# Where the modulation vectors are multiplied: from filler products of the tensor engine to VectorE accumulations

## Chip, core and metric

The kernel runs on one core of a Trainium2 chip. The metric is the device time of one execution in microseconds (us). The core has engines that run side by side and wait for one another by semaphores: TensorE (PE: products; PEld: its weight loads), VectorE (DVE), ScalarE (ACT), GpSimd (POOL), and SyncE (SP), which here issues all DMAs, in order.

## The reference

Two blocks of two layers each run over 256 tokens of 1024 channels, in float32. The first block has a pooling mixer, stick-breaking attention and two squared-relu MLPs. The second has windowed attention and differential attention, two more MLPs, and a context of 256 tokens. Every layer of the second block is modulated by vectors made from `c` and `c_ctx`:

```
for i in range(DEPTH):
    need_ctx = i < DEPTH - 1
    mod_x = jax.nn.silu(c) @ w_ada[i] + b_ada[i]
    mod_c = jax.nn.silu(c_ctx) @ w_ada[i] + b_ada[i]
    sh1, sc1, g1, sh2, sc2, g2 = jnp.split(mod_x[:, None, :], N_MOD, axis=-1)
    csh1, csc1, cg1, csh2, csc2, cg2 = jnp.split(mod_c, N_MOD, axis=-1)
    hx = x * (1.0 + sc1) + sh1
    hc = ctx * (1.0 + csc1) + csh1
...
```

`w_ada[i]` is 1024 x 6144, 25 MB for each of the two layers: two vectors times a large matrix. The change is in this product alone.

## The kernel before

Weights come from DRAM in blocks of 1 MB as two `raw` tiles (three buffers). ACT rounds a block to `whi`, DVE subtracts to make `wlo` (three buffers each), and PE multiplies activations, split in the same way, by three products for each pair (`mm`, L607). `mmf` (L613) is a product in full float32, `tr` (L637) a transpose by `ident`. An MLP has 16 blocks of hidden columns; for each, PE runs 48 products of 256 columns (up) and 24 of 512 columns (down), and ACT and DVE make the squared relu in `c` tiles between them.

The order of instructions on PE, DVE, ACT and POOL is decided when the program is built. Everything that PE does is written as *lanes*, generators that yield until an event, an instruction or a PSUM bank is there. `weave` runs the lanes, the first ready one first, with a table of costs for every engine; the other engines' instructions wait in lists and are laid down by the time at which they could start, less urgent ones (`urgent`) only if they are ready enough earlier. On the chip, each engine then runs its list strictly in order. All instructions of DVE, ACT, POOL and SP pass through one helper, so the profile shows them all at L109. Where PE would have nothing to do for more than 1 us, `keep_warm` lays down a product of `ident` with itself that nobody uses.

The product silu(c) @ w_ada was not a lane. `setup_rest` puts silu(c) and silu(c_ctx) into two of 32 columns of `cT` and queues two generators `ada(0)` and `ada(1)` as *fillers*. A filler step takes two `adaw` tiles (128 rows x 1024 columns of w_ada, 512 KB each, four buffers) and runs four products of 32 x 512 with `cT` as weights, each into its own quarter of one PSUM bank, summed over eight row blocks. `weave` takes a filler step where PE has a gap of over 300 ns, or where a step is due: `mlp` raises `due` after certain blocks (`F0`, `F1`, `F2`). There are 2 layers x 3 banks x 8 row blocks = 48 steps. After each bank, `ada_end` adds the bias, writes the gates to DRAM, transposes and fills `modT`, and marks the events `mod0.0` to `mod1.5`.

Of the kernel before, what the change touches and what calls it, by code (L numbers as in the profile page):

```python
# [11 lines left out]
F32 = mybir.dt.float32  # L12
# [8 lines left out]
P = 128  # L21
D = 1024
T = 256
# [10 lines left out]
# rows of the table of vectors that are laid along the partitions  # L34
# [21 lines left out]
FILL = 1000  # L56
# [4 lines left out]
# the gap of the tensor engine that is filled to keep its clock up; when it starts, and until when its clock is low  # L61
WARM = 1000
START, COLD = 1100, 6000
# how many fillers ahead of their time, and in which gaps
SPARE, GAP = -99, 300
# [4 lines left out]
F0, F1 = range(3, 15), range(2, 14)  # L70
F2 = {c: 2 for c in range(2, 14)}


class Unit:
    """to yield: a filler's next unit of work, once ops are through"""

    def __init__(self, ops):
        self.ops = ops


class Banks:
    """to yield: n PSUM banks are free, of the most that may be taken"""
# [5 lines left out]
class Op:  # L88
    """an instruction of an engine: what it waits for, what it takes, and when it ends (None: not laid down yet)"""
# [5 lines left out]
class Engine:  # L95
    """Stands for an engine: its calls are kept until the order of the engine's instructions is decided."""
# [58 lines left out]
class Net:  # L155
    """Everything that the tensor engine does is written as lanes: generators that yield after a few products, with the
    time until the lane's next products can start, the name of an event that it waits for, or the number of PSUM banks that
    it keeps between its steps. weave() runs the lanes, the
    first ready one first, and so lays down the tensor engine's order."""

    def __init__(self, ctx, tc, a, out):
# [19 lines left out]
        self.fill = deque()  # L181
        self.fill_at, self.fill_last, self.fill_wait, self.due = 0.0, 0.0, 0.0, 0
# [4 lines left out]
    def region(self, ap):  # L187
        """the name of what ap lies in, and its columns there as bits"""
# [53 lines left out]
    def ready(self, op):  # L242
        """when op can start for what it waits for; None: not known yet"""
# [14 lines left out]
    def first_op(self):  # L258
        """the instruction that starts next, (start, engine, op), of all engines"""
# [16 lines left out]
    def start(self, op, t, e):  # L276
        """when e can start op, which is ready at t; two engines don't go to a PSUM bank at once"""
# [28 lines left out]
    def settle(self, op):  # L306
        """lays down instructions until op is"""
# [30 lines left out]
    def done(self, *aps):  # L338
        """to yield: what lays aps down"""
# [18 lines left out]
    def fill_step(self):  # L358
        self.due -= isinstance(self.fill_wait, Unit)
        r = self.step(self.fill[0], 1)  # L360
        if r is None:
            self.fill.popleft()
        self.fill_last, self.fill_at, self.fill_wait = self.now, self.now + FILL, 0.0 if r is None else r

    def can_fill(self):
        t = self.when(self.fill_wait) if self.fill and self.now >= self.fill_at else None
        return t is not None and t <= self.now

    def when(self, r):
        """when a lane that yielded r goes on; None: not known yet"""  # L370
# [4 lines left out]
        if isinstance(r, Unit):  # L375
            r = r.ops
# [18 lines left out]
    def weave(self, lanes):  # L395
        lanes = [[g, 0.0] for g in lanes]
        while lanes:
            self.catch_up()
            self.sweep()
            if self.can_fill() and (self.due > 0 or not isinstance(self.fill_wait, Unit)):  # L400
                self.fill_step()
                continue
# [8 lines left out]
            else:  # L411
                if self.can_fill() and self.due > SPARE and (nxt is None or nxt - self.now > GAP):
                    self.fill_step()
                    continue
                n = self.first_op()
                ts = [t for t in (nxt, n and n[0], self.fill_at if self.fill and self.fill_at > self.now else None,
                                  self.when(self.fill_wait) if self.fill else None) if t is not None and t > self.now]
# [6 lines left out]
            r = self.step(e[0], 1 if e[0].__name__ in ("gemms", "setup_rest") else 0)  # L424
# [7 lines left out]
    def keep_warm(self):  # L432
        """a product that nobody asks for: the tensor engine's clock halves when it has been idle for some microseconds"""
# [11 lines left out]
    def need(self, name):  # L445
        while name not in self.ev:
            self.due = max(self.due, 1)
            yield 500

# [5 lines left out]
    def t(self, tag, cols, bufs, dt=F32):  # L455
        t = self.base.tile([P, cols], dt, name=self.uid(tag), tag=tag, bufs=bufs)
        if tag in ("raw", "adaw", "whi", "wlo"):
# [25 lines left out]
    def free(self, *banks):  # L483
        """nothing more will be asked of them"""
# [25 lines left out]
    def wide(self, src):  # L510
        """a vector in DRAM on every partition"""
# [42 lines left out]
    def block(self, key, w, c0, uses=1):  # L554
        """columns c0.. of w [1024, n] -> [128, 8, 256]"""
# [7 lines left out]
    def rows(self, key, w, c, uses=1):  # L563
        """rows 256 c.. of w [n, 1024] -> [128, 2, 1024]"""
# [50 lines left out]
    def sum3(self, out, l, r, n, last="l"):  # L615
        """out = the sum over k < n of l(k) @ r(k); the low parts of one side are used last"""
# [13 lines left out]
    def pairs(self, parts):  # L630
        """parts: (out, l's two parts, r's) on different rows of the array, in turns"""
# [18 lines left out]
    def meansq2(self, x):  # L650
        """the same of x [128, 1024], on two engines"""
# [5 lines left out]
    def meansq(self, src):  # L657
        """mean of the squares of each row of the two halves of 512 columns, as two parts of a sum"""
# [1365 lines left out]
```

## Time and profile before

| what | before |
|---|---|
| three runs | 1520.4, 1521.74, 1524.77 us |
| median | 1521.74 us |
| span of the profiled execution | 1520.4 us |
| HBM read in it | 257.18 MB |
| w_ada of it: 96 loads of 512 KB | 50.3 MB |

One execution is profiled. "Busy" is the time in which an engine had an instruction running; PE's ends are modelled. A chain of waits follows the work that ended last back to the start. A stretch A:B is a part of the span in us. In a group, "x384" is the number of instructions; a float32 product shows as two records on PE (a product of 32 x 512 likewise), so a filler step of four products shows as eight.

### The profile page before, as it was taken

The page shows a single profiled execution, that of the slowest core. Times are in us where ns is not written, and L with a number is a line of the kernel's source. Part 1 is how long each engine was busy: PE and PEld are TensorE (multiplying, and loading weights), DVE is VectorE, ACT ScalarE, POOL GpSimd, SP SyncE. Part 2 cuts the span into 40 slices and gives each one's busy share as a digit, 9 for nine tenths or more (in the row PEclk, how much of TensorE's full clock was granted, in tenths as well). Part 3 has the DMA queues.
Part 4 walks back from the last instruction along what each step waited for, and adds up shares of the span by engine and source line. Part 5 has one row for each costly group of instructions (what it writes and reads, how often), then busy time and mean ns, then how long its engine had stood idle before and what let it go on. Part 6 is the DMA issues. An engine that isn't in the chain of part 4 may idle for free.

```text
span 1520.4 us, 26084 instructions
## 1 busy us (share of the span) xinstructions
PE 1496.9 (98%) x10346; PEld 1316.7 (87%) x10346; DVE 980.2 (64%) x1939; ACT 744.5 (49%) x1565; POOL 37.8 (2%) x57
## 2 busy tenths in 40 slices
PE   8999999999999999999999999999999999999997
PEld 8878888988988888888799997878889999899996
DVE  7645558667766555888684443435479877885556
ACT  6544446565765554577542322222245544655442
POOL 2000000001000000000000000000000000100001
PEclk9999999999999999999999999999999999999999
DMA  8687778434656767644653234554224322366652
GB/s 291 221 273 275 241 250 277 144 120 149 199 148 217 230 216 235 213 164 137 209 183 98 84 111 162 172 168 165 84 85 138 97 71 84 98 208 193 187 182 90
DMA packets 152109, 261.02 MB, mean 172 GB/s; under 512 B 8985, under 2 KB 113906, under 8 KB 151986
## 3 DMA queue, kind: packets, MB, share of 16 engines
q1 hardware_dynamic: 151986, 259.35, 52.8%
q8 instruction: 81, 1.33, 0.4%
q14 instruction: 42, 0.34, 0.1%
HBM read 257.18 MB, written 2.13 MB: 171 GB/s over the span
## 4 chain that ended last, share of the span: by engine, by line
PE 87%; DVE 5%; DMA 5%; ACT 1%; issue 1%; SPq 0%; POOL 0%; ACTq 0%; DVEq 0%; POOLq 0%
PE b L607 77%; PE b L613 6%; PE b L637 4%; DVE wlo L109 2%; DMA adaw<-in_w_ada_dram 1%; DVE nat L109 1%; DVE c L109 1%; DMA raw<-in_w_up_dram 1%; DVE h L109 1%; DMA c<-in_b_lk_dram 1%; ACT whi L109 1%; DMA raw<-in_a_wq_dram 0%; ACT c L109 0%; DMA raw<-in_pool_w_dram 0%; DMA raw<-in_w_kv_dram 0%
## 5 line engine op out<-in xcount | busy, mean ns | idle before, releaser
L607 PE MATMUL b<-h,whi 128*128 128x256 f32 x3072 | 568.7, 284 | 0.0
L109 ACT CAST whi<-raw 128x512 fp32r<-128x512 f32 x716 | 400.8, 617 | 340.5 <-PE b L607 228.4
L109 DVE TENSOR_TENSOR wlo<-raw,whi 128x512 fp32r<-128x512 f32 x716 | 458.5, 687 | 159.3 <-ACT whi L109 157.7
L607 PE MATMUL b<-whi,c 128*128 128x512 f32 x1536 | 506.5, 396 | 0.0
L607 PEld LDWEIGHTS b<-h,whi 128*128 128x128 f32 x3072 | 483.8, 192 | 6.7 <-ACT c L109 2.5
L607 PE MATMUL b<-h,wlo 128*128 128x256 f32 x1536 | 378.6, 284 | 0.0
L607 PEld LDWEIGHTS b<-whi,c 128*128 128x128 f32 x1536 | 288.6, 188 | 88.2 <-ACT c L109 14.3
L607 PE MATMUL b<-wlo,c 128*128 128x512 f32 x768 | 300.3, 391 | 0.0
L607 PEld LDWEIGHTS b<-h,wlo 128*128 128x128 f32 x1536 | 294.2, 192 | 2.8 <-issue 0.3
L109 ACT ACTIVATE c<-b 128x512 f32<-128x512 f32 (+1 forms) x116 | 64.7, 568 | 226.3 <-PE b L607 224.5
L109 DVE TENSOR_TENSOR c<-c 128x512 f32<-128x512 f32 x80 | 55.2, 691 | 185.5 <-ACT c L109 185.2
L607 PE MATMUL b<-whi,h 128*128 128x256 f32 x896 | 170.6, 287 | 3.1 <-DVE c L109 2.7
L607 PEld LDWEIGHTS b<-wlo,c 128*128 128x128 f32 x768 | 144.6, 188 | 25.1
L607 PEld LDWEIGHTS b<-whi,h 128*128 128x128 f32 x896 | 141.8, 192 | 5.7 <-ACT c L109 3.7
L109 DVE TENSOR_TENSOR c<-b,c 128x512 f32<-128x512 f32 (+3 forms) x121 | 71.5, 597 | 99.4 <-PE b L607 69.6
L607 PE MATMUL b<-wlo,h 128*128 128x256 f32 x432 | 110.3, 288 | 0.0
L607 PEld LDWEIGHTS b<-wlo,h 128*128 128x128 f32 x432 | 83.6, 193 | 2.4 <-issue 1.5
L109 DVE TENSOR_TENSOR c<-c,c 128x512 fp32r<-128x512 f32 (+3 forms) x122 | 75.6, 633 | 8.2 <-ACT c L109 0.6
L109 ACT COPY c<-b 128x512 f32<-128x512 f32 (+1 forms) x78 | 44.9, 582 | 52.7 <-PE b L637 33.7
L637 PE MATMUL b<-ident,c 128*128 128x128 f32 x434 | 64.2, 275 | 3.4 <-DVE c L109 2.2
L109 ACT ACTIVATE c<-c 128x512 fp32r<-128x512 f32 (+1 forms) x112 | 64.7, 603 | 2.2
L637 PEld LDWEIGHTS b<-ident,c 128*128 128x128 f32 x434 | 49.3, 140 | 15.8 <-issue 5.5
(130 smaller groups left out, 982.0 us busy)
## 6 DMA issues: line engine op xcount, KB each, us to landing
raw<-in_mlp_w_dram SPq DMA_DIRECT2D x128, 512.0 KB
adaw<-in_w_ada_dram SPq DMA_DIRECT2D x96, 512.0 KB
raw<-in_w_up_dram SPq DMA_DIRECT2D x64, 512.0 KB
raw<-in_w_down_dram SPq DMA_DIRECT2D x64, 512.0 KB
raw<-in_w_kv_dram SPq DMA_DIRECT2D x16, 512.0 KB
raw<-in_a_wq_dram SPq DMA_DIRECT2D x16, 512.0 KB
raw<-in_a_wo_dram SPq DMA_DIRECT2D x16, 512.0 KB
raw<-in_w_q_dram SPq DMA_DIRECT2D x8, 512.0 KB
```

The source lines that it names most:

```text
L109: op, way = Op(), (self.cost(f, out, reads, kw), lambda: getattr(self.real, f)(out, *args, **kw))
L607: self.product(30 if free else max(n, 256) / 2.4 + 3, out, (l, r), lambda: self.pe.matmul(out, l, r, start=start, stop=stop, **k))
L613: self.product(30 if free else max(n, 128) / 0.6 + 4, out, (l, r), lambda: self.pe.matmul(out, l, r, start=start, stop=stop, **k))
L637: self.product(109, out, (src, self.ident), lambda: self.pe.transpose(out, src, self.ident))
```

## The change

The filler steps go, with `due`, `Unit`, `fills` and all that belongs to them. `ada` becomes a lane, which starts when `setup_rest` is through. For every 128 x 1024 tile of w_ada, DVE multiplies the tile by silu(c) of its row (one value for each partition) and adds it to an accumulator `acc`, and again for silu(c_ctx): at layer 1 only the first two of the six vectors are made for the context as well. After eight tiles an accumulator holds, on each partition, the sum over the row blocks. For each pair of vectors PE then sums over the partitions, by products with `rowsel`, whose column r is all ones. The `adaw` tiles have three buffers instead of four, `acc` has four, and a scratch area that is reserved for DMAs is made smaller to make room. DVE's instructions for it have urgency 3 (a smaller number goes first; the weights' roundings have 2, and less when their block is next).

```diff
         self.set_lam()
-        self.fill.extend(self.ada(i) for i in range(2))
-        self.fill_at = self.now + 8000
+        self.rowsel = c.tile([P, 2, 32], F32, name="rowsel")
+        nc.vector.memset(self.rowsel, 0.0)
+        for r in range(2):
+            nc.vector.memset(self.rowsel[:, r, r:r + 1], 1.0)
+        self.mark("ada")
...
-            raw = raws.popleft()
-            for jj in range(2):
-                j = 2 * i + jj
-                self.mmf(bank[32 * j:32 * j + 32, :], self.cT[:, k, :], raw[:, jj * 512:jj * 512 + 512], k == 0, k == 7, free=j > 0)
...
+                if k == 0:
+                    acc = [self.t("acc", 1024, 4) for _ in range(2 if layer == 0 or m < 2 else 1)]
+                    accs.append(acc)
...
+                raw = raws.popleft()
+                with self.urgent(ADAP):
+                    for r, t in enumerate(acc):
+                        g = self.cT[:, k, r:r + 1]
+                        if k == 0:
+                            nc.vector.tensor_scalar(t, raw, g, None, ALU.mult)
+                        else:
+                            nc.vector.scalar_tensor_tensor(t, raw, g, t, ALU.mult, ALU.add)
+                if n + ADAW < len(steps):
+                    raws.append(load(*steps[n + ADAW]))
+                if m % 2 == 0 or k < 7:
+                    yield self.done(*acc)
+                    continue
+                yield self.done(*acc), Banks(1)
                 bank = self.bank()
...
+                for r in range(len(acc)):
+                    for j in range(4):
+                        self.mmf(bank[32 * j:32 * j + 32, :], self.rowsel[:, r, :], accs[j // 2][r][:, j % 2 * 512:j % 2 * 512 + 512],
+                                 r == 0, r == len(acc) - 1, free=j > 0)
+                yield from self.ada_end(layer, m // 2, bank, bias)
...
-            self.due += fills.get(c, 0)
...
-            if self.can_fill() and (self.due > 0 or not isinstance(self.fill_wait, Unit)):
-                self.fill_step()
-                continue
...
-    nc = bacc.Bacc("TRN2", target_bir_lowering=False, num_devices=1)
+    nc = bacc.Bacc("TRN2", target_bir_lowering=False, num_devices=1, dynamic_dma_scratch_size=1024)
```

Since the costs in `weave` decide the order, it moves everywhere. Three places show it.

PE in the first MLP, at the down products of one block, before (`b_658` and `b_659` are accumulators, `b_962` the fillers' bank; "x2" are equal rows):

```order
L607 MATMUL b_658<-whi_1406,c_1404 128x512
L607 MATMUL b_658<-wlo_1407,c_1404 128x512
L607 MATMUL b_658<-whi_1406,c_1405 128x512
L613 MATMUL b_962<-adaw_1297,cT 32x512 x2
L613 MATMUL b_962<-adaw_1300,cT 32x512 x2
L607 MATMUL b_659<-whi_1406,c_1404 128x512
L607 MATMUL b_659<-wlo_1407,c_1404 128x512
```

And now (`mm` is at L573 of the changed kernel):

```order
L573 MATMUL b_658<-whi_1401,c_1399 128x512
L573 MATMUL b_658<-wlo_1402,c_1399 128x512
L573 MATMUL b_658<-whi_1401,c_1400 128x512
L573 MATMUL b_659<-whi_1401,c_1399 128x512
L573 MATMUL b_659<-wlo_1402,c_1399 128x512
```

The filler step is gone from between the products. In its stead there are, at one place of this MLP, two rows for each of `acc_843`, `acc_1384`, `acc_844` and `acc_1385` with `rowsel`.

DVE in the first MLP before, two blocks (`wlo` of the weights, then the two `c` rows of the squared relu):

```order
L109 TENSOR_TENSOR wlo_1823<-raw_1824,whi_1822 128x512 x2
L109 TENSOR_TENSOR wlo_1823<-raw_1825,whi_1822 128x512 x2
L109 TENSOR_TENSOR c_1883<-c_1882 128x512
L109 TENSOR_TENSOR c_1885<-c_1883,c_1884 128x512
L109 TENSOR_TENSOR wlo_1887<-raw_1888,whi_1886 128x512 x2
L109 TENSOR_TENSOR wlo_1887<-raw_1889,whi_1886 128x512 x2
```

And now (all of DVE's instructions are at L98 of the changed kernel):

```order
L98 TENSOR_TENSOR c_1752<-c_1750,c_1751 128x512
L98 SCALAR_TENSOR_TENSOR acc_1385<-adaw_1484,cT,acc_1385 128x1024
L98 TENSOR_TENSOR wlo_1754<-raw_1755,whi_1753 128x512 x2
L98 TENSOR_TENSOR wlo_1754<-raw_1756,whi_1753 128x512 x2
L98 SCALAR_TENSOR_TENSOR acc_1384<-adaw_1582,cT,acc_1384 128x1024
L98 SCALAR_TENSOR_TENSOR acc_1385<-adaw_1582,cT,acc_1385 128x1024
L98 SCALAR_TENSOR_TENSOR acc_1384<-adaw_1657,cT,acc_1384 128x1024
L98 TENSOR_TENSOR wlo_1798<-raw_1799,whi_1797 128x512 x2
L98 TENSOR_TENSOR wlo_1798<-raw_1800,whi_1797 128x512 x2
L98 TENSOR_TENSOR c_1864<-c_1863 128x512
```

Four accumulations stand among the ten instructions of a block. Of the 160 in all, 49 are laid down among the `wlo` that belong to 60 to 240 us of the profile before, 33 among those of 240 to 390, 53 of 390 to 600, 9 of 600 to 770 and 16 at the start of the third MLP. Layer 1's begin beside the second MLP and end early in the third; the last filler step before starts at 1067 us, near the third MLP's end.

PE at the end of the first MLP before (the last down product, then the transposes of the normalised activations for keys, values and queries):

```order
L607 MATMUL b_661<-whi_2292,c_2358 128x512
L613 MATMUL b_1787<-adaw_2137,cT 32x512 x2
L613 MATMUL b_1787<-adaw_2140,cT 32x512 x2
L637 MATMUL b_2496<-ident,c_2424 128x128 x4
L637 MATMUL b_2506<-ident,c_2425 128x128 x4
L613 MATMUL b_1787<-adaw_2254,cT 32x512 x2
L613 MATMUL b_1787<-adaw_2257,cT 32x512 x2
L637 MATMUL b_2527<-ident,c_2515 128x128 x4
```

And now (L579 with `ident` alone is a keep-warm product, L603 a transpose):

```order
L573 MATMUL b_661<-whi_2290,c_2358 128x512
L579 MATMUL b_2494<-ident 128x128
L579 MATMUL b_2496<-ident 128x128
L579 MATMUL b_2500<-ident 128x128
L579 MATMUL b_2502<-ident 128x128
L579 MATMUL b_2504<-ident 128x128
L579 MATMUL b_2507<-ident 128x128
L579 MATMUL b_2512<-ident 128x128
L579 MATMUL b_2514<-ident 128x128
L579 MATMUL b_2517<-ident 128x128
L603 MATMUL b_2522<-ident,c_2429 128x128 x4
L603 MATMUL b_2529<-ident,c_2430 128x128 x4
```

Where filler steps stood, nine keep-warm products stand before the transposes, and four more follow until the stage is under way: 13, against one before. In the whole program they are 69 against 58.

More of the change, by code (lines that the diff above doesn't have):

```diff
@@ L62 @@
 WARM = 1000
+ADAW, ADAP = 3, 3
 START, COLD = 1100, 6000
-SPARE, GAP = -99, 300
 LATE = {"so": 2, "co": 2, "xo": 2, "do": 2}
 FIN = lambda tok, ks: [(h, k) for h in range(2) for k in ks] if tok else [(h, k) for k in ks for h in range(2)]
[L70 to L78, printed above, removed]
 class Banks:
@@ L356, in urgent @@
         self.prio = old
[L358 to L367, printed above, removed]
     def when(self, r):
@@ L411, in weave @@
             else:
-                if self.can_fill() and self.due > SPARE and (nxt is None or nxt - self.now > GAP):
-                    self.fill_step()
-                    continue
                 n = self.first_op()
-                ts = [t for t in (nxt, n and n[0], self.fill_at if self.fill and self.fill_at > self.now else None,
-                                  self.when(self.fill_wait) if self.fill else None) if t is not None and t > self.now]
+                ts = [t for t in (nxt, n and n[0]) if t is not None and t > self.now]
                 assert ts, [e[1] for e in lanes]
@@ L423, in weave @@
                 continue
-            r = self.step(e[0], 1 if e[0].__name__ in ("gemms", "setup_rest") else 0)
+            r = self.step(e[0], 1 if e[0].__name__ in ("gemms", "setup_rest", "adas") else 0)
             if r is None:
@@ L456, in t @@
         t = self.base.tile([P, cols], dt, name=self.uid(tag), tag=tag, bufs=bufs)
-        if tag in ("raw", "adaw", "whi", "wlo"):
+        if tag in ("raw", "adaw", "acc", "whi", "wlo"):
             old = self.tags.setdefault(tag, [])
@@ L735, in mask, with ada @@
         return mk
[L738 removed]
+    def ada(self):
         nc = self.nc
[L740 to L770 removed]
@@ new lines, in ada, with load @@
+        for layer in range(2):
+            w = self.a["w_ada_2"][layer].rearrange("(k p) f -> p k f", p=P)
+            b = self.a["b_ada_2"][layer]
+            steps = [(m, k) for m in range(6) for k in range(8)]
+            def load(m, k):
+                raw = self.t("adaw", 1024, ADAW)
+                nc.sync.dma_start(raw, w[:, k, m * 1024:m * 1024 + 1024])
+                return raw
+            raws = deque(load(*s) for s in steps[:ADAW])
+            for n, (m, k) in enumerate(steps):
+                if m % 2 == 0 and k == 0:
+                    accs = []
+                    bias = self.c()
+                    nc.vector.memset(bias, 0.0)
+                    bv = b[m * 1024:m * 1024 + 2048].rearrange("(j f) -> j f", f=512)
+                    for j in range(4):
+                        nc.sync.dma_start(bias[32 * j:32 * j + 2, :], bv[j:j + 1, :].broadcast_to((2, 512)))
+                if k == 0:
+                    acc = [self.t("acc", 1024, 4) for _ in range(2 if layer == 0 or m < 2 else 1)]
+                    accs.append(acc)
+                    for t in acc:
+                        self.uses[t.name] = 2
+                raw = raws.popleft()
[12 more added lines that the diff above has]
+                yield self.done(*acc), Banks(1)
+                bank = self.bank()
+                for r in range(len(acc)):
+                    for j in range(4):
+                        self.mmf(bank[32 * j:32 * j + 32, :], self.rowsel[:, r, :], accs[j // 2][r][:, j % 2 * 512:j % 2 * 512 + 512],
+                                 r == 0, r == len(acc) - 1, free=j > 0)
+                yield from self.ada_end(layer, m // 2, bank, bias)
@@ L919, in fold, with mlp @@
         return G, B
-    def mlp(self, name, h, waits, done, fills={}, hc=None, hc_waits=(), cacc=None, extra={}):
+    def mlp(self, name, h, waits, done, hc=None, hc_waits=(), cacc=None, extra={}):
         nc = self.nc
@@ L1839, in gemms @@
             G[1](), G[2]()
-            yield from self.mlp("m0", H["m0"], ("m00", "m01"), done, fills={c: 1 for c in F0})
+            yield from self.mlp("m0", H["m0"], ("m00", "m01"), done)
             self.stickmask = self.mask("stick", 640)
@@ L1848, in gemms @@
             done = residual("m1", a["mlp_post_g"][1])
-            yield from self.mlp("m1", H["m1"], ("m10", "m11"), done, fills={c: 1 for c in F1},
+            yield from self.mlp("m1", H["m1"], ("m10", "m11"), done,
                                 extra={3 * b: [lambda b=b: self.ctx_q(H["hc"], b, st)] for b in (1, 2, 3)})
```

38 lines of the change are left out of this document (5 added, 33 removed).

## The prediction, made before the changed kernel ran

> **What bounds the kernel now.** I read the page first: the shares of the engines and the chain that ended last.
>
> ```profile
> span 1520.4 us, 26084 instructions
> ...
> PE 1496.9 (98%) x10346; PEld 1316.7 (87%) x10346; DVE 980.2 (64%) x1939; ACT 744.5 (49%) x1565; POOL 37.8 (2%) x57
> ...
> PE 87%; DVE 5%; DMA 5%; ACT 1%; issue 1%; SPq 0%; POOL 0%; ACTq 0%; DVEq 0%; POOLq 0%
> ```
>
> The tensor engine (PE) carries 87% of the chain, VectorE (DVE) and the DMAs 5% each. A mean says little about a stage, so next come the chain in order of time (start, length, what) and the engines' busy time in seven stretches, cut at the changes of stage.
>
> ```profile
> 122.13 11.44 PE b L607 x72
> 134.56 11.44 PE b L607 x72
> ...
> 770.52 146.92 PE b L607 x963
> ...
> 1330.47 179.54 PE b L607 x1152
> ```
>
> ```profile
> core 0: us, PE busy (x) PEld busy (x) DVE busy (x) ACT busy (x) POOL busy (x), PEclk, DMA share, GB/s
> 60.00:240.00 180.00, 179.56 (x1151) 146.93 (x1150) 99.14 (x170) 83.02 (x160) 2.19 (x4) 1.00 0.77 255
> 240.00:390.00 150.00, 148.61 (x1136) 135.97 (x1134) 105.37 (x207) 94.93 (x210) 4.02 (x4) 1.00 0.52 164
> 390.00:600.00 210.00, 210.00 (x1492) 180.92 (x1491) 128.71 (x263) 116.38 (x260) 0.00 (x0) 1.00 0.65 205
> 600.00:770.00 170.00, 166.21 (x1221) 139.78 (x1219) 137.43 (x315) 113.74 (x261) 4.96 (x10) 0.99 0.54 181
> 770.00:1120.00 350.00, 350.00 (x2264) 306.79 (x2257) 172.72 (x274) 101.57 (x182) 0.00 (x0) 1.00 0.41 135
> ```
>
> The four MLPs are pure PE time: the last one's 1152 products run in one piece of 179.54 us, 11.22 us for each of 16 blocks of 72. In the first MLP, blocks start 134.56 - 122.13 = 12.43 us apart. The 1.21 us between them are a filler step. DVE stands idle there for 180 - 99.1 = 80.9 us, but only for 44.6 us in the key/value and stick-breaking stretch and 32.6 us in the windowed attention (600 to 770).
>
> **What goes: 48 filler steps of PE.** The group of the steps' products, one step in the first MLP, and the steps in the stretches:
>
> ```profile
> L613 PE MATMUL b<-adaw,cT x384: 592/605/617, 72.7 to 1067.6; 128*32 128x512 f32 x192
> ```
>
> ```profile
> 133.18 0.39 PE L607 MATMUL b<-whi,c 128*128 128x512 f32 x1
> 133.50 1.07 PE L613 MATMUL b<-adaw,cT 128*32 128x512 f32 x8
> 134.49 0.50 PE L607 MATMUL b<-whi,c 128*128 128x512 f32 x1
> ```
>
> ```profile
> 60.00:240.00 180.00, 18.09 (x128) 2.65 (x128) 1.00 0.77 255
> ...
> 390.00:600.00 210.00, 9.59 (x72) 1.41 (x72) 1.00 0.65 205
> 600.00:770.00 170.00, 11.18 (x80) 1.70 (x80) 0.99 0.54 181
> 770.00:1120.00 350.00, 14.37 (x112) 2.04 (x104) 1.00 0.41 135
> ```
>
> The three views are the step's group over the whole run, the timeline round one step, and the steps' share of each stretch. Eight records make a step: 48 in all. From start to start the step holds PE for 134.49 - 133.50 = 0.99 us, and the products on either side are spread by another 0.2 us; the two block pitches give the same sum, 1.21. So 16 steps lie in 60 to 240, 9 in 390 to 600, 9 before 770, and 14 in the third MLP (one of them across the cut at 770). The third MLP runs without a break where it has no steps (146.92 us), so nothing but PE sets its time.
>
> Not all 16 steps of the first stretch are on the path. The last three stand at the MLP's end:
>
> ```profile
> 231.25 1.06 PE L613 MATMUL b<-adaw,cT 128*32 128x512 f32 x8
> 232.25 1.09 PE L637 MATMUL b<-ident,c 128*128 128x128 f32 x8
> 233.27 1.07 PE L613 MATMUL b<-adaw,cT 128*32 128x512 f32 x8
> ...
> 238.17 1.06 PE L613 MATMUL b<-adaw,cT 128*32 128x512 f32 x8
> ```
>
> Transposes of normalised activations stand between them, and the order of the changed kernel has 13 keep-warm products here, where the one before has 1. I take it that these three filled time in which PE had nothing else. So 13 + 9 + 14 = 36 steps count in full: 36 x 1.21 = **43.6 us**. Of the other 12 (at most 14.5 us, at least nothing), the nine in windowed attention stand where DVE is busy 137.4 of 170 us and several engines wait on each other; I count a third of the nine, **3.6 us**, and none of the three.
>
> **What comes to PE.** 40 products of the same shape with `rowsel` as weights, in six groups: 16 records each for layer 0's three groups and layer 1's first, 8 for the other two. That is ten step lengths of 1.00 and six times 0.21 for the edges: **11.3 us**, of which 2.2 us fall to each of the first four groups (one in the first MLP, one in stick-breaking, two in the second MLP). PE's net is 43.6 + 3.6 - 11.3 = 35.9 us.
>
> **What comes to DVE.** 160 instructions on 128x1024: 140 SCALAR_TENSOR_TENSOR and 20 TENSOR_SCALAR. No row of before has that width. The nearest have half and a quarter of it (groups with their mean in ns, and two in a row in the timeline):
>
> ```profile
> L109 DVE SCALAR_TENSOR_TENSOR c<-x,s_rs,wide 128x512 f32<-128x512 f32 x16 | 11.4, 746 | 2.1 <-POOL s_rs L109 2.0
> ...
> L109 DVE SCALAR_TENSOR_TENSOR h<-b,poolg,h 128x256 fp32r<-128x256 f32 x8 | 3.6, 473 | 0.8 <-ACT h L109 0.8
> ```
>
> ```profile
> L109 DVE TENSOR_SCALAR c<-c,s_rz 128x512 f32<-128x512 f32 x20 | 9.3, 482 | 0.3
> ...
> L109 DVE TENSOR_SCALAR c<-c,s_rz 128x256 f32<-128x256 f32 x23 | 7.5, 352 | 0.6
> ```
>
> ```profile
> 26.06 1.41 DVE L109 SCALAR_TENSOR_TENSOR x<-nat,s_rs,x 128x512 f32<-128x512 f32 x2
> ```
>
> Doubling the width again: 746 + 2 x 273 = 1292 ns and 482 + 2 x 130 = 742 ns. Two in a row take 1.41 us, so a neighbour starts after 1.41 - 0.75 = 0.66 us, 0.09 before the end that the record shows. I use 1.20 us (at least twice 0.66 less a start, at most 1.29) and 0.66 us: 140 x 1.20 + 20 x 0.66 = 181 us, DVE's share rising to about 77%.
>
> The order puts them early: 49 beside the first MLP (42 + 7), 33 in 240 to 390 (28 + 5), 53 in 390 to 600 (48 + 5), 9 to 770, 16 at the start of the third MLP. In time 55.0, 36.9 and 60.9 us in the first three. DVE's idle there, with PE's net change taken off, is 80.9 - 13.5 = 67.4, 44.6 + 2.2 = 46.8 and 81.3 - 6.5 = 74.8 us. So 82, 79 and 81% of all idle time has to serve. What the idle consists of (who waited for what: total, times, longest):
>
> ```profile
> DVE c L109 <- ACT c L109: 224.0, 102, 7.1
> ...
> DVE wlo L109 <- ACT whi L109: 157.7, 107, 6.3
> ```
>
> ```profile
> SPq L109 <- DVE wlo L109: 927.9, 317, 22.8
> SPq L109 <- PE b L613: 163.9, 43, 12.5
> ```
>
> Its pieces have means of 2.2 and 1.5 us: one new instruction fits a mean piece, with a rest. That makes three quarters usable, with half and all as ends. A late `wlo` hurts only once PE has used up the weight blocks made ahead (three buffers, 5.6 us of PE each), while in attention PE waits for the `c` behind it. With three quarters, 4.4 + 1.8 + 4.8 = **11.0 us** do not fit; with all nothing; with half 21.3 + 13.5 + 23.5 = 58.3 us. A new wait comes with it: each new instruction waits for its `adaw` load, and behind it in DVE's fixed order stand `wlo` and, in attention, the `c` of the next step, for which PE waits. The sums' own wait, PE for the last accumulation, sits at six places alone; if DVE is late there, that is part of the same sum.
>
> **Queues.** Behind an `adaw` load in SP's queue stand weight loads. Its wait for a buffer was for PE's steps (163.9 us) and is now for two DVE instructions; the queue waits 927.9 us for `wlo` anyway, so I cost it at nothing while DVE keeps up, and it is part of the same 58 us if not. Traffic: 24.5 loads instead of 32 beside the first MLP leave 45.9 - 3.9 = 42.0 MB in 166.5 us, 252 GB/s against 255. The other two stretches rise to some 220 and 235, below what the first sustains. `rowsel`, the bias and the smaller scratch cost nothing here: one-time, or beside idle time of 80.9 us.
>
> **Sum.** 1520.4 - 35.9 + 11.0 = **1495 us**. The span is 1520.4, as is the fastest of the three runs; the median 1521.74 is 0.1% above.
>
> **Rivals.**
> (1) *DVE takes PE's place* (slower). From 60 to 600 us DVE's stream has no room; `wlo` and the attention's `c` come late and PE waits. It decides below a usable share of (152.8 - 35.9) / 189.0 = 62%. At half: 1520.4 - 35.9 + 58.3 = 1543 us; at 55%, 1533. For it: 82% must serve, in a fixed order in which DVE also waits for ACT and for loads. Against: pieces longer than one instruction.
> (2) *Everything hides*, and the steps in attention pay too: 1520.4 - (43.6 + 14.5 - 11.3) = 1474 us.
> (3) *The steps lay in slack* and removing them brings nothing: 1520 us. Against it stand 12.43 and 11.22 us. [...]
> (4) *The clock drops* where no step fills a pause. One drop is in the trace:
>
> ```profile
> 648.00:652.00 4.00, 1.33 (x12) 0.79 (x5) 2.04 (x4) 3.09 (x9) 0.00 (x0) 0.89 0.87 279
> 652.00:656.00 4.00, 4.00 (x26) 4.00 (x26) 3.94 (x9) 3.82 (x10) 0.00 (x0) 0.68 0.83 305
> ```
>
> PE was busy 1.33 of 4 us, then the granted clock read 0.89 and 0.68: 4 x (0.11 + 0.32) = 1.7 us lost. At all 12 places, 20 us: 1515 us. The keep-warm products speak against it. [...]
>
> **Chances.** Forecast (65 to 90% usable, 1480 to 1515): 0.50. Rival 1: 0.24, of which 0.03 lies near the turning point. Rival 2: 0.14. Rival 3: 0.07. Rival 4: 0.05, split over both sides of the bound. About 0.3% (4.6 us) can be told from no change, so faster means below 1517. Faster 0.50 + 0.14 + 0.02 = 0.66; within 0.07 + 0.03 + 0.03 = 0.13; slower 0.21. The range goes from rival 2 to rival 1 at 55%, 1473 to 1533, and leaves out the worse half of rival 1.
>
> **What would show it.** Right: blocks of the first and third MLP 11.2 to 11.6 us apart; DVE near 1.2 us an instruction and over 90% busy from 60 to 600; the third MLP shorter by 16 us. Wrong: PE idle before products with `wlo` or `c`, ended by DVE, adding up to more than 36 us before 640 us (rival 1); blocks still 12.4 us apart (rival 3); more stretches with a clock under 0.9 (rival 4). The forecast also fails if the wide instruction takes much over 1.3 us.

## The result, and the profile after

| kernel | median of its runs | range | ratio to before, 95% interval |
|---|---|---|---|
| before, same chip | 1521.13 us (4 runs) | 1520.4 to 1524.77 | 1 |
| changed | 1480.9 us (4 runs) | 1479.58 to 1481.3 | 0.9727 [0.9713, 0.9741] |

The changed kernel is faster by 40 us, more than the 26 us forecast, and inside the range. One of the seven runs of the kernel before that stood beside e1 to e4 took 1618.24 us at a mean granted clock of 0.85; medians and ratios leave it out. The page of its profiled execution (span, busy time of each engine, shares of the chain that ended last):

```profile
span 1479.5 us, 25724 instructions
...
PE 1452.4 (98%) x10064; PEld 1313.7 (89%) x10064; DVE 1154.4 (78%) x2100; ACT 745.7 (50%) x1567; POOL 38.7 (3%) x57
...
PE 89%; DVE 5%; DMA 3%; ACT 2%; issue 1%; POOL 0%; SPq 0%; ACTq 0%; DVEq 0%; POOLq 0%
```

PE is busy 44.5 us less than the 1496.9 us before, DVE 174.2 us more, and DVE's share of the chain is still 5%: nearly all of the new work lies beside PE's. The same stretches as before:

```profile
core 0: us, PE busy (x) PEld busy (x) DVE busy (x) ACT busy (x) POOL busy (x), PEclk, DMA share, GB/s
60.00:240.00 180.00, 177.19 (x1163) 160.56 (x1162) 166.36 (x243) 91.21 (x171) 3.34 (x4) 1.00 0.79 254
240.00:390.00 150.00, 148.76 (x1119) 132.70 (x1119) 136.85 (x243) 97.66 (x222) 2.49 (x4) 1.00 0.63 204
390.00:600.00 210.00, 208.98 (x1456) 185.62 (x1455) 190.26 (x318) 115.14 (x256) 1.41 (x2) 1.00 0.74 239
600.00:770.00 170.00, 166.17 (x1241) 146.85 (x1241) 157.09 (x334) 115.33 (x261) 4.34 (x8) 1.00 0.51 166
770.00:1120.00 350.00, 349.96 (x2272) 319.74 (x2272) 204.67 (x333) 114.08 (x211) 3.79 (x8) 1.00 0.37 119
```

DVE now runs 91 to 92% of the time from 60 to 600 us, and PE 98% and more beside it. The chain in order of time (start, length, what) has the first and third MLP in whole pieces, where blocks and filler steps took turns before:

```profile
62.53 100.30 PE b L573 x645
...
810.95 274.53 PE b L573 x1752
```

The new instructions by form (least, median and greatest ns; first and last start), and all that PE waited for between 60 and 640 us (total, times, longest):

```profile
L98 DVE SCALAR_TENSOR_TENSOR acc<-adaw,cT,acc x140: 1274/1278/1289, 66.2 to 805.8; 128x1024 f32<-128x1024 f32 x140
...
L579 PE MATMUL b<-acc,rowsel x80: 592/592/617, 162.8 to 807.6; 128*32 128x512 f32 x80
L98 DVE TENSOR_SCALAR acc<-adaw,cT x20: 629/747/754, 64.9 to 789.5; 128x1024 f32<-128x1024 f32 x20
```

```profile
PE b L603 <- DVE c L98: 3.2, 5, 1.0
PE b L573 <- DVE wlo L98: 1.7, 3, 1.2
PE b L573 <- DVE c L98: 1.7, 3, 0.9
```

The durations were sized well (1278 and 747 ns against 1292 and 742; neighbours start 1.20 us apart, as assumed). PE's waits for DVE come to 6.6 us, where 36 would have meant that DVE had become the bound. The keep-warm products, which stand where PE would wait, add little to that: they take 3.6 us from 60 to 700 us, against 0.9 before. PE's 80 records of sums stand in six groups, at 162.8, 286.4, 447.8 and 567.7 us (1.92 us each from first start to last end) and at 727.7 and 807.2 us (1.07 us): 9.8 us in all.

To see where the 41 us of the trace came from, I number the 4608 products of `h` with `whi` or `wlo` that each trace has in the order of their starts, and compare the start of the same product in both. The differences are cumulative; the points are named by the time before.

| point before, us | stage there | changed kernel ahead by | gained since the last point | forecast for it |
|---|---|---|---|---|
| 202 | late in the first MLP | 13.8 | 13.8 | |
| 244 | its end, on to keys and values | 12.1 | -1.7 | 9.1 for both |
| 382 | stick-breaking done | 10.5 | -1.6 | -4.0 |
| 582 | second MLP done | 19.0 | 8.5 | 3.9 |
| 770 | windowed attention done | 25.2 | 6.2 | 1.4 |
| 1101 | third MLP done | 40.6 | 15.4 | 14.5 |

The forecasts are the prediction's terms, each put where its step or sum stands (up to 582: 9 x 1.21 - 2.2 - 4.8 = 3.9). The prediction counted the fourth sum to the second MLP, but it comes after that MLP's last product, so it stands in the row of 770, and so does the step at 769.5 us, the first of the third MLP's 14. One entry is good to about 1.6 us: a second profile of the changed kernel (e11) is ahead by 13.6, 12.2, 10.5, 18.2, 26.0 and 41.2 us at the same points, and one of the kernel before (e10, with the same instructions in the same order) is 1.2 us ahead of the first at 202 us and stays so, since the filler step at 83 us does not wait 1.2 us for its w_ada load there. The third MLP came out nearly as forecast. In the first two MLPs and windowed attention the kernel gained more than forecast, in stick-breaking it lost less. Two suspects: the loss to DVE's late results was set too high, or more of the 48 steps paid than 36.

### The profile page after: what moved, and what is told of

It reads as the page before. It is cut to its first block, busy times and chain, and to the rows that moved or that the text cites. A ratio compares the mean times of both kernels' runs of the same rounds, so it can differ in the third digit from the quotient of the medians.

```text
span 1479.5 us, 25724 instructions
## 1 busy us (share of the span) xinstructions
PE 1452.4 (98%) x10064; PEld 1313.7 (89%) x10064; DVE 1154.4 (78%) x2100; ACT 745.7 (50%) x1567; POOL 38.7 (3%) x57
## 3 DMA queue, kind: packets, MB, share of 16 engines
q1 hardware_dynamic: 151986, 259.35, 54.5%
## 4 chain that ended last, share of the span: by engine, by line
PE 89%; DVE 5%; DMA 3%; ACT 2%; issue 1%; POOL 0%; SPq 0%; ACTq 0%; DVEq 0%; POOLq 0%
PE b L573 81%; PE b L579 4%; PE b L603 3%; DVE c L98 1%; DVE wlo L98 1%; DVE nat L98 1%; ACT c L98 1%; ACT whi L98 1%; DVE h L98 1%; DMA raw<-in_a_wq_dram 1%; DMA raw<-in_pool_w_dram 0%; DMA raw<-in_w_down_dram 0%; DVE s_mx L98 0%; POOL s_rs L98 0%; DMA adaw<-in_w_ada_dram 0%
## 5 line engine op out<-in xcount | busy, mean ns | idle before, releaser
L573 PE MATMUL b<-h,whi 128*128 128x256 f32 x3072 | 568.3, 284 | 0.0
L98 ACT CAST whi<-raw 128x512 fp32r<-128x512 f32 x716 | 403.2, 618 | 313.1 <-PE b L573 177.8
L98 DVE TENSOR_TENSOR wlo<-raw,whi 128x512 fp32r<-128x512 f32 x716 | 458.3, 687 | 53.8 <-ACT whi L98 52.4
L573 PE MATMUL b<-whi,c 128*128 128x512 f32 x1536 | 497.1, 393 | 0.9 <-DVE c L98 0.9
L573 PEld LDWEIGHTS b<-h,whi 128*128 128x128 f32 x3072 | 483.7, 192 | 5.3 <-issue 1.8
L573 PE MATMUL b<-h,wlo 128*128 128x256 f32 x1536 | 379.4, 284 | 0.0
L573 PEld LDWEIGHTS b<-whi,c 128*128 128x128 f32 x1536 | 288.6, 188 | 63.7 <-issue 3.6
L573 PE MATMUL b<-wlo,c 128*128 128x512 f32 x768 | 300.2, 391 | 1.4 <-DVE wlo L98 1.4
L573 PEld LDWEIGHTS b<-h,wlo 128*128 128x128 f32 x1536 | 294.2, 192 | 3.5 <-issue 0.7
L98 ACT ACTIVATE c<-b 128x512 f32<-128x512 f32 (+1 forms) x116 | 64.9, 568 | 229.4 <-PE b L573 218.8
L98 DVE SCALAR_TENSOR_TENSOR acc<-adaw,cT,acc 128x1024 f32<-128x1024 f32 x140 | 176.0, 1279 | 2.7 <-DMA adaw<-in_w_ada_dram 2.5
L573 PEld LDWEIGHTS b<-wlo,c 128*128 128x128 f32 x768 | 144.5, 188 | 28.1 <-DVE wlo L98 2.2
L573 PE MATMUL b<-whi,h 128*128 128x256 f32 x896 | 168.2, 286 | 0.1
L98 DVE TENSOR_TENSOR c<-c 128x512 f32<-128x512 f32 x80 | 55.1, 690 | 138.4 <-ACT c L98 138.3
L573 PEld LDWEIGHTS b<-whi,h 128*128 128x128 f32 x896 | 140.5, 191 | 1.8 <-issue 1.1
L98 DVE TENSOR_TENSOR c<-b,c 128x512 f32<-128x512 f32 (+3 forms) x121 | 71.5, 596 | 66.2 <-PE b L573 48.7
L573 PE MATMUL b<-wlo,h 128*128 128x256 f32 x432 | 109.8, 288 | 0.4 <-DVE wlo L98 0.3
L573 PEld LDWEIGHTS b<-wlo,h 128*128 128x128 f32 x432 | 82.6, 191 | 3.1 <-issue 1.5
L98 DVE TENSOR_TENSOR c<-c,c 128x512 fp32r<-128x512 f32 (+3 forms) x122 | 75.9, 634 | 7.7
L603 PE MATMUL b<-ident,c 128*128 128x128 f32 x434 | 64.5, 276 | 7.4 <-DVE c L98 5.7
L98 ACT COPY c<-b 128x512 f32<-128x512 f32 (+1 forms) x78 | 44.7, 582 | 47.3 <-PE b L603 27.8
L98 ACT ACTIVATE c<-c 128x512 fp32r<-128x512 f32 (+1 forms) x112 | 64.8, 603 | 2.2
```

The costliest lines, as they stand in the source:

```text
L98: op, way = Op(), (self.cost(f, out, reads, kw), lambda: getattr(self.real, f)(out, *args, **kw))
L573: self.product(30 if free else max(n, 256) / 2.4 + 3, out, (l, r), lambda: self.pe.matmul(out, l, r, start=start, stop=stop, **k))
L603: self.product(109, out, (src, self.ident), lambda: self.pe.transpose(out, src, self.ident))
```

## The experiments

Differences below are to the kernel before run on the same chip; its medians were 1521.89 us (e1 to e4), 1522.28 (e5 to e8) and 1522.73 (e9 to e12). Line numbers move by a few where lines were added (L575 is L573, L581 is L579).

**e1, accumulations of 64 columns.** The order is still built with the cost of 1024, so the engines' lists stay. The other 960 columns of each of the 140 accumulations are left out; the 20 TENSOR_SCALAR that begin a sum keep all of theirs. In the traces, the order on PE, DVE, ACT and POOL is that of the changed kernel.

```diff
+    if out.name.startswith("acc_"):
+        n = 1024
...
-                            nc.vector.scalar_tensor_tensor(t, raw, g, t, ALU.mult, ALU.add)
+                            nc.vector.scalar_tensor_tensor(t[:, 0:64], raw[:, 0:64], g, t[:, 0:64], ALU.mult, ALU.add)
```

> The changed kernel with the same order on PE, DVE, ACT and POOL (SP's loads move by a place or two), but each of the 140 SCALAR_TENSOR_TENSOR works on 64 of the 1024 columns, so the modulation is not the reference's. DVE loses about 140 us of work. If the 11 us that the prediction allowed for late DVE instructions were really paid, the time falls from 1480.9 to about 1470 us. If all of DVE's new work hides beside other work, it stays at 1479 to 1482 us, although DVE's share falls from 78% to about 68%.

Measured: 1478.24 us, ratio 0.9713 [0.9698, 0.9729]. The instructions shrank from 1278 to 278 ns, which takes 140 us off DVE, and the kernel gained 2.7 us by the medians, 3.4 by the spans (1476.1 against 1479.5); the intervals overlap. It is 19.9 us ahead of before at 582 and 27.5 at 756, where the changed kernel has 19.0 and 24.1 in its first trace and 18.2 and 24.9 in its second. So up to 582 us, for which I had allowed 11 us, the length of the accumulations costs 0.9 us by the one and 1.7 by the other, and in windowed attention 2.5 or 0.9: little in both places, and not to be divided more finely.

**e2, every accumulation twice**, the second time with a factor column of zeros, in an order built for it.

```diff
                             nc.vector.scalar_tensor_tensor(t, raw, g, t, ALU.mult, ALU.add)
+                            nc.vector.scalar_tensor_tensor(t, raw, self.cT[:, k, 2:3], t, ALU.mult, ALU.add)
```

> The changed kernel with every SCALAR_TENSOR_TENSOR made twice, the second time with a column of zeros as factor, so that the result is the same; the order is planned anew. DVE gets about 170 us more, some 1320 us in all. By the rival that DVE takes PE's place below a usable share of 62%, the first 600 us are now far over DVE's room and the time rises by 50 us or more, unless the plan moves the work later. If DVE's idle time can be used nearly whole, the accumulations spread into the third MLP, where DVE is idle for half of the time, and the time rises by less than 10 us.

Measured: 1539.61 us, ratio 1.0116 [1.01, 1.0132]: 59 us more than the changed kernel. That is the rise of 50 us or more which I expected from the rival, but not for its reason, a general lack of room: up to 582 us this kernel is 23.6 us ahead of before, more than the changed one (two sums have run by then instead of three). All is lost near 740. PE's busy share is 98% here too; the loss stands inside it. The group of keep-warm products (records | busy us, mean ns | idle before) in the changed kernel, then in e2, then e2's timeline on PE:

```profile
L579 PE MATMUL b<-ident 128*128 128x128 f32 x138 | 18.0, 278 | 0.6 <-DVE h L98 0.6
```

```profile
L579 PE MATMUL b<-ident 128*128 128x128 f32 x636 | 74.5, 276 | 0.6 <-DVE h L98 0.6
```

```profile
723.75 40.92 PE L579 MATMUL b<-ident 128*128 128x128 f32 x365
764.60 1.05 PE L579 MATMUL b<-acc,rowsel 128*32 128x512 f32 x4
770.40 1.93 PE L579 MATMUL b<-acc,rowsel 128*32 128x512 f32 x8 [4.75 <-DVE acc L98]
```

PE runs 56.5 us more of products that nobody uses, 40.92 us of them in one piece that ends at the third sum of layer 0. That sum comes at 447.8 us in the changed kernel; here it comes at 764.6, when the third MLP already needs the vectors `mod0.4`. From 727 to 766 us DVE starts 34 accumulations, one every 1.16 us, and nothing else. The loss is a missed due time.

**e3, the kernel before with thin steps**, in its own order: the seven later products of a sum have 64 columns instead of 512.

```diff
-                self.mmf(bank[32 * j:32 * j + 32, :], self.cT[:, k, :], raw[:, jj * 512:jj * 512 + 512], k == 0, k == 7, free=j > 0)
+                cols = 512 if k == 0 else 64
+                o, l, v = bank[32 * j:32 * j + 32, 0:cols], self.cT[:, k, :], raw[:, jj * 512:jj * 512 + cols]
+                self.product(30 if j > 0 else 512 / 0.6 + 4, o, (l, v), lambda: self.pe.matmul(o, l, v, start=k == 0, stop=k == 7))
```

> The kernel before with the same order on PE, DVE, ACT and POOL, but the filler products of the last seven of the eight row blocks have 64 columns instead of 512, so the modulation is not the reference's. 42 of 48 steps shrink from 0.99 us to perhaps 0.2. DVE gets nothing. If 36 of 48 steps are on the path, as predicted, the time falls by 42 x 0.8 x 36/48 = 25 us, to about 1496. If all pay, by 34 us, to about 1488. If they lay in slack, it stays at 1521. In the stretch of windowed attention (nine steps) the prediction's third means 2 us, all of them 7 us.

Measured: 1494.43 us, ratio 0.9815 [0.9798, 0.9833], 27.5 us less than before. By the sum alone this is nearer to 36 paying steps than to 48. The places say more. In the trace, a thinned step on a free path holds PE for 0.25 us from start to start instead of 1.00, so it can save 0.75; six steps, the first of each bank, stay whole. By the count of products, the thinned steps saved 6.7 us in the first MLP up to 202 (ten of them, 0.67 each), 5.1 in the second (seven, 0.73), **6.2 from there to 770** (nine, 0.69; the eight in windowed attention 5.7 up to 756), and 9.0 in the third MLP (twelve, 0.75). The passage from 202 to 244 has four and gains 0.8, no more than the first of them, still in the MLP's blocks, can save. So those in windowed attention pay about as much as any, the three at the MLP's end nothing that can be told: 45 steps pay, 39 of them thinned.

**e4, layer 1 only from the third MLP on**, out of windowed attention, where e1, beside the first trace, seemed to have found DVE's loss.

```diff
+            if layer == 1:
+                yield "m2 started"
```

> The changed kernel with the lane held before layer 1's accumulations until the third MLP has begun, so that 64 of the 160 move from the second MLP and windowed attention to where DVE is about half idle. If late DVE instructions cost something in the second MLP and in attention (4.8 us and more by the prediction), the time falls by 4 to 8 us. If DVE's work hides there, it stays within 1.5 us of 1480.9.

Measured: 1480.24 us, ratio 0.9725 [0.971, 0.974]. Windowed attention gains 11.8 us (18.6 ahead at 582, 30.4 at 770) instead of 6.2, the third MLP 11.2 instead of 15.4. Three groups of sums, 1.92 + 1.07 + 1.06 us, now stand in the third MLP, where PE has no slack and the changed kernel has one of 1.07: that is 3.0 of the 4.2 us less. As a whole the time stays within the 1.5 us that I gave for hidden work; what is left is too small to be told from the changed kernel.

**e5, an order that doesn't know the accumulations' length.** On the chip they keep their 1024 columns.

```diff
+    if out.name.startswith("acc_"):
+        n = 64
```

> The changed kernel; when the order is built, every operation on acc is costed as if it had 64 columns (some 0.19 us) instead of its true 1024 (1.19 us); on the chip it keeps its full width. Theory 'room by planning' (the 180 us of VectorE work cost PE only some 3 us because the order knows their length and lays them where nobody waits for VectorE): late VectorE work costs PE 8 to 15 us more, 1489 to 1496 us. Rival 'slack' (late VectorE results are absorbed since PE has products of other lanes and of the three weight blocks ahead): within 3 us of the changed kernel, 1478 to 1484 us.

Measured: 1553.27 us, ratio 1.0202 [1.0178, 1.0226]: slower than before, and 72 us above the changed kernel, nearly five times the most that I had expected. PE's waits and three stretches:

```profile
PE b L575 <- DVE wlo L98: 30.8, 13, 5.4
PE b L575 <- DVE c L98: 13.4, 3, 5.6
```

```profile
60.00:240.00 180.00, 157.04 (x913) 136.71 (x912) 172.18 (x225) 65.95 (x121) 0.00 (x0) 0.91 0.80 259
240.00:390.00 150.00, 128.04 (x917) 113.72 (x916) 135.31 (x204) 72.31 (x154) 3.40 (x4) 0.93 0.69 223
390.00:600.00 210.00, 205.02 (x1440) 179.08 (x1439) 170.09 (x321) 125.06 (x288) 3.35 (x4) 0.98 0.67 215
```

This is the rival "DVE takes PE's place" as the prediction drew it: PE waits for `wlo`, and for the `c` of the attention. From 60 to 700 us its records leave 50.0 us of gaps against 8.7 in the changed kernel. The granted clock falls as well: 180 x 0.09 + 150 x 0.07 + 210 x 0.02 = 30.9 us. By the clock's records without rounding it is 29.0 us, of which 24.7 fall while PE runs and the rest into the gaps, which are counted already. So 41.3 + 24.7 = 66 of the 73 us between the two spans. DVE is busy 172 us in the first stretch, only six more than in the changed kernel, but 99 of them are accumulations, against 59.

**e6, only layer 1's accumulations twice**, to test the due time of e2.

```diff
+                            if layer == 1:
+                                nc.vector.scalar_tensor_tensor(t, raw, self.cT[:, k, 2:3], t, ALU.mult, ALU.add)
```

> The changed kernel; each accumulation of layer 1's modulation alone is followed by a second one with a factor column of zeros (56 more of 1.28 us, 72 us of VectorE, from about 455 us on). Theory 'deadline' (doubling all of them lost 58 us over the changed kernel because layer 0's last vectors, due at the third MLP's start, came late; layer 1's are due from 1100 us on): within 3 us of the changed kernel, 1478 to 1484 us. Rival 'room' (each added accumulation costs where VectorE is full, wherever it lies): 56 of 140, so four tenths of 58 us, about 23 us, 1504 us.

Measured: 1479.67 us, ratio 0.9717 [0.9692, 0.9742]. 56 more accumulations, 72 us of DVE, cost nothing where nothing is due before about 1100 us. The due time stands, the rival falls.

**e7, no steps at the end of the first MLP.** There the changed kernel had lost 1.7 us. DVE's timeline in it:

```profile
213.66 0.69 DVE L98 TENSOR_TENSOR nat<-b,wide 128x512 f32<-128x512 f32 x1
214.27 1.41 DVE L98 SCALAR_TENSOR_TENSOR x<-nat,s_rs,x 128x512 f32<-128x512 f32 x2
215.59 0.75 DVE L98 TENSOR_SCALAR acc<-adaw,cT 128x1024 f32<-128x1024 f32 x1
216.39 0.69 DVE L98 TENSOR_TENSOR nat<-b,wide 128x512 f32<-128x512 f32 x1
217.00 0.20 DVE L98 TENSOR_SCALAR s_ms<-s_ss,s_ss 128x1 f32<-128x1 f32 x1
217.19 0.69 DVE L98 TENSOR_TENSOR wlo<-raw,whi 128x512 fp32r<-128x512 f32 x1
218.32 1.41 DVE L98 SCALAR_TENSOR_TENSOR c<-x,s_rs,wide 128x512 f32<-128x512 f32 x2 [0.44 <-POOL s_rs L98]
```

An `acc` and a `wlo` stand among the steps from the residual (`nat`, `x`) to the `c` that PE transposes next.

```diff
             for n, (m, k) in enumerate(steps):
+                if layer == 0 and n == 23:
+                    yield "x.m01"
```

> The changed kernel; layer 0's steps from the 24th on (its accumulation at 206 us) wait until the first MLP's residual is written for both tokens, so no accumulation lies in that MLP's last 12 us. Theory 'order at the stage's end' (the passage from the first MLP's last product to the next stage is 1.7 to 2.9 us longer in the changed kernel because accumulations and the wlo they delay stand among the residual's VectorE steps): 1.5 to 3 us under the changed kernel, 1478 to 1479.4 us, gained between 202 and 244 us. Rival 'only a new order' (the passage is long for another reason): within 1 us of the changed kernel.

Measured: 1480.8 us, ratio 0.9725 [0.9704, 0.9745]: no gain. The passage from 202 to 244 us did lose its extra 1.7 us, but from 244 to 382 the kernel gave 3.1 us back where the changed one gave 1.6. The held accumulations come later (the second sum at 292.5 us instead of 286.4) and the time is only moved. My theory named the place rightly and its worth wrongly.

**e8 and e12, hold and late layer 1 together; e11, the changed kernel again.** The diff is that of e4 and e7 together.

> The hold of the run before, and layer 1's steps start with the third MLP. If both effects add (the passage after the first MLP 1.5 to 3 us shorter; windowed attention 5 us shorter against 4 lost in the third MLP): 1476 to 1478.5 us, under both kernels. If the gains are only moved: 1479 to 1482 us.

> The changed kernel itself, beside the next run on the same chip: 1479 to 1482 us.

> The hold at the first MLP's end with layer 1's steps from the third MLP on, once more beside the changed kernel: 2 to 3 us under it (1477 to 1479 us) if the trace's 2.9 us is the order's; within 1 us of it if that was one execution's chance.

Measured: 1478.6 us (e8, ratio 0.9717 [0.9693, 0.974]), then 1481.37 (e12, 0.9727 [0.9706, 0.9748]) beside 1480.82 for the changed kernel (e11, 0.973 [0.9709, 0.9751]). The 2 us of the first run did not come again. No version here beats the changed kernel.

**e9, accumulations go first.** Their length is known, but their rank is 0 in place of 3.

```diff
-ADAW, ADAP = 3, 3
+ADAW, ADAP = 3, 0
```

> The changed kernel; the accumulations' rank in the order is 0 in place of 3, so where an accumulation and a weight's wlo or a stage's step could go, the accumulation goes first unless it would start 0.4 us later; their length is costed truly. Theory 'known length' (it is enough that the order knows how long each takes, since products are then laid where VectorE's results will be there): 1478 to 1486 us. Rival 'rank' (what keeps the loss small is that accumulations stand behind everything else): at least half of the 72 us that the run with the wrong length lost, 1510 us and more, with PE waiting for wlo again.

Measured: 1524.43 us, ratio 1.0014 [1.0002, 1.0026]. All of the gain is gone, 44 us of it through the rank alone. "Known length" falls. From 60 to 640 us PE waits 7.7 us for `wlo` and 11.4 for `c`, where the changed kernel has 1.7 and 4.9. PE's timeline has a pause of 3.10 us before a product of `whi` with `c`; DVE's timeline shows what the `c` stood behind:

```profile
229.24 1.22 PE L573 MATMUL b<-whi,c 128*128 128x512 f32 x2 [3.10 <-DVE c L98]
```

```profile
220.44 0.68 DVE L98 TENSOR_TENSOR wlo<-raw,whi 128x512 fp32r<-128x512 f32 x1
221.04 0.68 DVE L98 TENSOR_TENSOR c<-c 128x512 f32<-128x512 f32 x1
221.64 0.68 DVE L98 TENSOR_TENSOR wlo<-raw,whi 128x512 fp32r<-128x512 f32 x1
222.24 0.68 DVE L98 TENSOR_TENSOR c<-c,c 128x512 fp32r<-128x512 f32 x1
222.84 2.49 DVE L98 TENSOR_TENSOR wlo<-raw,whi 128x512 fp32r<-128x512 f32 x4
225.25 1.28 DVE L98 SCALAR_TENSOR_TENSOR acc<-adaw,cT,acc 128x1024 f32<-128x1024 f32 x1
226.45 0.68 DVE L98 TENSOR_TENSOR c<-c 128x512 f32<-128x512 f32 x1
227.28 1.30 DVE L98 TENSOR_TENSOR wlo<-raw,whi 128x512 fp32r<-128x512 f32 x2 [0.15 <-ACT whi L98]
228.50 0.69 DVE L98 TENSOR_TENSOR c<-c,c 128x512 fp32r<-128x512 f32 x1
```

The `c` that PE wants starts at 228.50 and ends at 229.19. Between it and the `c` step at 222.24 stand six `wlo`, an `acc` and one more `c` step, and nine accumulations start in the 14 us ahead of these rows. The first two stretches:

```profile
60.00:240.00 180.00, 170.49 (x1014) 143.75 (x1013) 173.89 (x235) 78.38 (x145) 1.52 (x1) 0.98 0.81 266
240.00:390.00 150.00, 141.70 (x1008) 121.55 (x1007) 144.85 (x222) 83.39 (x178) 2.53 (x3) 0.99 0.71 229
```

As in e5, DVE is only a little busier (174 against 166 us), but takes 92 us of accumulations in the first stretch instead of 59, and less of everything else. Of the 44 us, 15.6 are more gaps between PE's records from 60 to 700 us (24.3 against 8.7), 8.9 more keep-warm products in the whole run (26.9 against 18.0), and 6.3 the lower clock while PE ran; the other 13 I could not put to a cause.

**e10, the kernel before with the smaller DMA scratch** alone.

```diff
+    nc = bacc.Bacc("TRN2", target_bir_lowering=False, num_devices=1, dynamic_dma_scratch_size=1024)
```

> The kernel before with one part of the change alone: the 1024 bytes given as the DMA scratch size. No theory gives it a cost: 1519 to 1524 us, and the same order on every engine. If it moved the time, the change's 41 us would not all belong to the steps.

Measured: 1521.78 us, ratio 0.9998 [0.9985, 1.0012]. This part of the change has no effect that can be told.

## Why the prediction was right in direction and 16 us off

The likeliest case held in its mechanism: PE sheds the steps and DVE takes them up beside it. The sum was 16.0 us short in the trace (1495.5 against 1479.5), from three terms:

- **The nine steps in windowed attention, counted as a third (3.6 us): mis-sized.** All nine pay, 10.9 us at 1.21 each (by e3, in which the eight thinned ones save 5.7 of 6.0 us). DVE's 137 of 170 busy microseconds there had made me expect PE to wait anyway; but the steps were laid as work on PE's own path, and taking them out moved everything behind them forward. 7.3 us.
- **The 11.0 us for DVE's lack of room: mis-sized, and wrongly reasoned.** With all else as measured, 54.5 (45 steps) - 9.8 (sums) - 40.9 leaves 3.8 us, a remainder that holds the scatter between traces too; e1 puts 2.7 to 3.4 of it to the accumulations' length. By place, steps less sums less gain come to 2.9 us at the first MLP's end and 2.9 (1.3 in e11) in windowed attention, where I had allowed nothing, and to about nothing in stick-breaking and the second MLP, charged with 1.8 and 4.8. In the three stretches that I charged, the accumulations take 159.5 us and leave DVE 46.5 idle: 77% of the room used, at little cost. The rows on DVE's idle pieces were of the whole run; from 60 to 600 us both have a mean of 1.7 us (113.2 us in 66 pieces, 64.2 in 37), so an instruction still fits one. "Three quarters usable" charged a loss for fit to a placement that was itself the outcome of fitting: 51, 31 and 53 accumulations stand in the stretches because an order that knows their length and ranks them behind the rest laid no more there. e5 takes away the one and e9 the other. Then the accumulations crowd in (99 and 92 us of the first stretch, over 90% of the room) and the loss is 72 and 44 us. The runs do not separate the crowding from what brings it about. 7.3 us.
- **The sums, 11.3 us: mis-sized.** A group of 16 records holds PE 1.92 us, not 2.2, one of eight 1.07. 1.5 us.

7.3 + 7.3 + 1.5 = 16.1. Right as they stood: 36 steps at 1.21, nothing for the three at the first MLP's end (e3), the third MLP shorter by 15.4 (16 forecast), blocks of 72 products 11.2 us apart (100.30 / 645 x 72 in the first MLP), instruction lengths, queues and traffic at nothing (254, 204 and 239 GB/s beside 252, 220 and 235), and the clock (rival 4 didn't come: 1.00 in all stretches of the changed kernel).

Rival 1 was priced on the right wait, but from a share of room that the order itself sets: the same 160 instructions cost 3.8 us, 44 more with another rank (e9) and 72 more with a wrong length (e5). A sum that misses its due time costs besides (e2). Rival 2, at 1474 us, came closest in time: its premise of hidden accumulations nearly held, and of its 12 further steps nine paid. For the question here, whether the steps pay, PE's busy share of 98% read truer than the weight loads' 87%: 45 of 48 paid. But in e2 its 98% hid 56 us of unused products.

Not settled: the 13 us of e9 above, and what the changed kernel loses in windowed attention. Ten steps up to 770 us make 12.1; e4 and e6 gain 11.8 and 12.0 there, e12 and e8 12.9 and 13.3. The changed kernel has two sums there that those four have later (3.0 us), and of the 9.1 that remain it gains 6.2, in e11 7.8. These 1.3 to 2.9 us came with the order and not with the amount of DVE's work, since e6 has more of that (16 accumulations from 600 to 770 us against 11).

## What to carry to other kernels

Here, work that moved from the bound engine to one with idle time was worth nearly its whole price (40.9 us of the 44.7 that 45 steps less the sums come to) where it ranked behind everything else, with its length known, and was done by the time it was due; count the room, but look at who must wait for whom before charging for fit. Where a scheduler sets the order, its cost of the new instruction is part of the change: a wrong length turned 40 us of gain into 31 of loss. A tensor engine that is "98% busy" can be idling in keep-warm products (74.5 us of them in e2), so read their group before the share.

## What the runs showed of the hardware that was not expected

The clock's answer to a pause. In e5 two pauses of PE have the same length, 3.43 us, with different ends. Windows from the first pause's start, then from the second's:

```profile
114.29:116.29 2.00, 0.00 (x1) 0.00 (x0) 2.00 (x2) 1.52 (x3) 0.00 (x0) 1.00 0.99 315
116.29:118.29 2.00, 0.56 (x1) 0.50 (x2) 2.00 (x5) 1.14 (x2) 0.00 (x0) 0.56 0.69 205
118.29:120.29 2.00, 2.00 (x6) 1.58 (x5) 2.00 (x4) 0.00 (x0) 0.00 (x0) 0.50 0.77 262
```

```profile
254.80:258.23 3.43, 0.00 (x1) 0.00 (x1) 3.43 (x5) 2.18 (x4) 0.00 (x0) 1.00 0.60 197
258.23:262.23 4.00, 4.00 (x24) 1.95 (x25) 3.55 (x6) 0.58 (x2) 0.00 (x0) 1.00 0.85 238
```

After the first the granted clock is 0.50 for 6.8 us, after the second it stays at 1.00. A pause of only 1.98 us (at 167.93) was followed by 0.50, one of 2.71 us (at 182.99) by nothing. So length alone does not tell.

The clock's own records tell more. The eleven drops of e5 between 60 and 1450 us begin whole multiples of 3.41 us apart (those at 116.54, 157.50, 171.15 and 218.94 us are 0, 12, 16 and 30 such periods from the first of them) and last one period or two. Cut into these periods, the same pauses look different (two periods from each of the pauses of 3.43, 1.98, 2.71 and 3.43 us):

```profile
113.13:116.54 3.41, 1.16 (x5) 0.56 (x3) 3.41 (x4) 2.68 (x6) 0.00 (x0) 1.00 0.96 327
116.54:119.95 3.41, 2.23 (x5) 1.82 (x6) 3.41 (x6) 1.14 (x2) 0.00 (x0) 0.50 0.71 222
167.74:171.15 3.41, 1.43 (x11) 1.17 (x10) 3.41 (x5) 0.00 (x0) 0.00 (x0) 1.00 0.79 217
171.15:174.57 3.42, 3.42 (x18) 3.42 (x18) 3.42 (x5) 1.14 (x2) 0.00 (x0) 0.50 0.91 268
181.39:184.81 3.42, 1.60 (x12) 1.32 (x10) 3.42 (x4) 1.14 (x2) 0.00 (x0) 1.00 0.79 225
184.81:188.22 3.41, 2.52 (x20) 2.46 (x21) 3.41 (x5) 1.14 (x2) 0.00 (x0) 1.00 0.73 231
253.08:256.49 3.41, 1.72 (x8) 1.10 (x6) 3.31 (x5) 1.86 (x5) 0.00 (x0) 1.00 0.68 212
256.49:259.90 3.41, 1.67 (x14) 0.71 (x18) 3.41 (x6) 1.49 (x3) 0.00 (x0) 1.00 0.75 224
```

The second pause of 3.43 us was split into 1.69 and 1.74 us of idle time, that of 2.71 us into 1.82 and 0.89; 2.25 us of the first, and all 1.98 of the short one, fell into one period. In e5, each of the ten periods at full clock in which PE was idle for 1.91 us or more was followed by 0.50, and none with 1.74 us or less; of two between, 1.80 was and 1.82 was not. In e9 one with 1.66 us was. So in e5 the idle time within one period set the pauses that a drop followed apart from the others, with 1.80 and 1.82 us too close to tell; the 1.66 us of e9 lie below 1.69 and 1.74 us that no drop followed in e5. The pause of 1.98 us cost PE half of the 3.42 us after its period, 1.7 us.
